# A two-layer decoder trunk on one core: PSUM tiles split by drain time, branch blocks merged in twos, attention one gate sooner, weight units asked for one ahead

## The chip, the core and the metric

The kernel runs on one NeuronCore of a Trainium2 chip. The core has a matrix engine (TensorE, PE in the profile), a vector engine (VectorE, DVE), a scalar engine (ScalarE, ACT), a general engine (GpSimd, POOL), and a queue that starts transfers (SyncE, SP). Each runs its own list of instructions in order and waits on semaphores for the others. Matrix products land in PSUM, which the kernel deals out in tiles of one or two banks; a bank holds 128 x 512 float32 numbers. The metric is the time of one execution on the device, in microseconds (us). It is given as the median of several runs, and beside it stands one profiled execution with its span, the time from its first to its last instruction.

## The reference

Each of two layers is a half-weighted feed-forward block, a mixing block with two branches, and a second feed-forward block. The sequence has 256 positions and the model 1024 features; everything is float32. The chunked selection of key blocks in the full text reduces, at 256 positions and one key block of 256, to causal attention over that block.

```python
def hybrid_layer(x, ...):
    x = x + 0.5 * swiglu(rms_norm(x, ffn1_norm), ffn1_w_gate_up, ffn1_w_down)   # 1024 -> 2 x 2816 -> 1024
    h = rms_norm(x, mix_norm)
    z = h @ w_in                                                                # u, q, k, v: 512 each; gates: 2048
    u, q, k, v, gl = z[..., :o1], z[..., o1:o2], z[..., o2:o3], z[..., o3:o4], z[..., o4:]
    y_pool = multiscale_pool(u, pool_w, pool_scale)      # trailing means over 2, 4, 8, 16 minus u, mapped per group
    q = rope(rms_norm(q.reshape(B, S, N_HEADS, HEAD_DIM), q_norm))              # 8 heads of 64
    k = rope(rms_norm(k.reshape(B, S, N_HEADS, HEAD_DIM), k_norm))
    y_attn = moba_attention(q, k, v)
    gates = jax.nn.sigmoid(gl + b_gate).reshape(B, S, N_BRANCH, D)
    merged = gates[:, :, 0] * (y_pool @ w_branch_pool) + gates[:, :, 1] * (y_attn @ w_branch_attn)
    x = x + merged @ w_out
    return x + 0.5 * swiglu(rms_norm(x, ffn2_norm), ffn2_w_gate_up, ffn2_w_down)
```

## The kernel before

**Numbers.** Every float32 operand of the large products is split into a high part that TensorE's float32r format holds and the rest as a low part. A product is then three: high by high, high by low, low by high. `chain` (L108) makes one 128-block of such a product with two matmuls: the weight's high part against both parts of the activation (N = 512, the two results side by side in one bank), and the weight's low part against the high part (N = 256, added to the first half). A bank thus ends as two halves of 256 columns, and whoever drains it adds them. `drain` (L129) does so: ScalarE copies the second half, and VectorE adds the first.

**Weights.** They come in units of 1 MB (`unit`, L67): SyncE starts a load into one of four `raw` buffers, ScalarE writes the high parts (L91) and VectorE the low parts (L92), in two halves of 128 x 1024, each into one of six `hl` tiles. A call of `unit` brings a unit and returns its halves; for three units before the program's start, loading is written out (L542 to L569), and the calls take these from the list `ahead`.

**PSUM.** The pool `pmm` has two tiles of two banks, `pat` has four of one bank. Waits go by tile: who writes any part of a tile waits for all who had to read an earlier content of any of its parts, and two halves of a tile that are drained at different times hold each other up.

**A layer.** `ffn` (L244): 22 pairs of blocks (`pair`: 32 matmuls into a `pmm` tile, then `drain` into a tile `ab`), each followed by the product with the norm r (L265), the SiLU and a split; then eight output blocks of 22 chains each, added to x by `add_x` (L282). The norm r itself is computed in the middle of the second pair (`norm_all`), or, in the program's first ffn, at the end of three pairs that run together (`pairs`). Then `mix` (L424): q, k, v (`tokens`, `normed`) and the pooling input u; eight gate pairs (`gate`), between which the small work is set; two times four branch blocks, each of 12 matmuls from the pooling branch (`pk`) and 12 from the attention branch (`yk`), merged with the sigmoids of the gates by `merge` (L496) into `mk`; and eight output blocks (w_out). Then the second ffn. The small work among the gates is pooling (`pool`, VectorE and a little GpSimd), the transposes of q and k (`to_features`), the scores and the softmax of four pairs of heads (`scores`), the transposes of the softmax's result (`by_key`, tile pT), and its products with v (`heads_end`). `pl`, `pr`, `pT`, `sq`, `sw`, `ab` and `mg` share one tag of five buffers.

**Order.** TensorE's order is that of the program text (`manual_schedule` for PE). For ScalarE and VectorE a scheduler sets the order when the kernel is built, from the program's order and its own estimates.

The lines that bear on what follows: the two-bank tiles for w_out's first four blocks are

```python
pss = [t[c] for t in big() for c in range(2)]     # 524: outputs 0, 1 in one tile, 2, 3 in the other
```

and in the branch the first four blocks use the same form (L508), the next four a one-bank tile each (L510).

Of the kernel before, what the change touches and what calls it, by code (L numbers as in the profile page):

```python
# [39 lines left out]
def trunk_kernel(ctx: ExitStack, tc: tile.TileContext, x_in, w_in, pw_in, qkn_in, rope_in, mask_in, band_in, out):  # L40
# [178 lines left out]
    def norm_tok():  # L219

        st = pat.tile([P, 2], F32, name="st", tag="at")
        for t in range(2):
            mm(st[:, t:t + 1], lhsT=acc[:, t * P:(t + 1) * P], rhs=ones[:, :1], start=True, stop=True)
        rt = small.tile([P, 2], F32, name="rt", tag="rt", bufs=2)
        rsqrt(rt, st, 1.0 / D)
        return rt

    def spread(rt):
# [3 lines left out]
        halves(dr, dg.rearrange("p a b -> p (a b)"))  # L232
        st = pat.tile([P, S], F32, name="st", tag="at")
        for j in range(2):
# [8 lines left out]

    def ffn(after, first=False):  # L244
        gs = []
# [5 lines left out]
        for i in range(NF):  # L251
# [4 lines left out]
            if first and i == 2:  # L256
                r.append(pairs([unit() for _ in abs_], [t for _, t in abs_], norm_all))
            elif not first and i == 1:
                pair(unit(), ab, NK // 2, lambda: r.append(norm_all()))
            else:  # L260
                pair(unit(), ab)
# [27 lines left out]
    def tokens(pss, mid=None):  # L289

        for kh in range(2):
            hl = unit(tok=True)
            for t in range(2):
                ts = slice(t * P, (t + 1) * P)
                for kk in range(4):
                    k = kh * 4 + kk
                    for c in range(2):
                        z = chunks(hl[kk // 2])[:, kk % 2 * 2 + c]
                        ps = pss[t][c]
                        prod(ps, hx[:, k, 0, ts], z, k == 0, False)  # L300
# [3 lines left out]

    def normed(pss, rt, name):
        z = acts.tile([P, 2, GW], F32, name=name, tag="tok", bufs=3)
        for t in range(2):
            rc = rt[:, t:t + 1]
            for c, ps in enumerate(pss[t]):
                zc = z[:, t, c * S:(c + 1) * S]  # L310
                act(zc, ps[:, 1, :], AF.Copy, scale=rc)
                stt(zc, ps[:, 0, :], rc, zc, op0=OP.mult, op1=OP.add)
        return z
# [110 lines left out]
    def mix(l, after):  # L424
# [21 lines left out]

        ps = big()
        tokens(ps, lambda: box.update(rt=norm_tok()))
        rt = box["rt"]
        q = normed(ps, rt, "q")  # L450
        ps = little()
        tokens(ps)
        k = normed(ps, rt, "k")
        norm_rope(q, qkn[:, l, 0])
        ps = big()
        tokens(ps, lambda: box.update(r=spread(rt)))
        v = normed(ps, rt, "v")
        norm_rope(k, qkn[:, l, 1])
        ps = [pat.tile([P, 2, S], F32, name="pu", tag="at") for _ in range(4)]
        for kh in range(2):  # L460
            hl = unit()
            for kk in range(4):
                i = kh * 4 + kk
                for g in range(4):
                    chain(ps[g], hl, kk * 4 + g, hk[i], i == 0, i == NK - 1)
# [20 lines left out]
        pw = pool_weights(l)  # L486
        gate(5)
        pool_map(pw, d, pk, l)
        gate(6)
        pTs[2] = [by_key(pr) for pr, _ in prs[2]]  # L490
        prs[3] = scores(qT, kT, 3)
        gate(7)
        heads_end(2)
        ei = prs[NP - 1][1][1]

        def merge(f, ps):  # L496
            mg = tmp.tile([P, 2, S], F32, name="mg", tag="t512", bufs=5)
            with tc.issue_after(ei.ins):
                for j in range(2):
                    c = C_BG + j * NK + f  # L500
                    act(gates[:, f, j, :], gates[:, f, j, :], AF.Sigmoid, bias=gain[:, l, c:c + 1])
            tt(mg, ps, gates[:, f], op=OP.mult)  # L502
            tt(mg[:, 0, :], mg[:, 0, :], mg[:, 1, :], op=OP.add)
            halves(mk[f], mg[:, 0, :])

        for f0 in (0, 4):
            if f0 == 0:
                pss = [t[c] for t in big() for c in range(2)]  # L508
            else:
                pss = [pat.tile([P, 2, S], F32, name="ps", tag="at") for _ in range(4)]  # L510
            us = []
            for e in range(4):
                if e % 2 == 0:
                    us.append(unit())
                if f0 == 0 and e == 3:
                    heads_end(3)
                chain3(pss[e][:, 0], us[-1], e % 2 * 8, pk)
                if f0 == 0 and e == 0:
                    pTs[3] = [by_key(pr) for pr, _ in prs[3]]
# [4 lines left out]
        pss = [t[c] for t in big() for c in range(2)]  # L524
        for ks in (range(6), range(6, NK)):
# [44 lines left out]
    for l in range(L):  # L570
        ffn(lambda f: prep(f, l, C_GM), l == 0)
        if l == 0:
# [3 lines left out]
        if l + 1 < L:  # L576
            ffn(lambda f: prep(f, l + 1, C_G1))
        else:
            ffn(lambda f: nc.sync.dma_start(out[:, f, :], x[:, f, :]))

# [89 lines left out]
```

## Time and profile before

| | us |
|---|---|
| median of 3 runs | 1034.88 (1033.51 to 1035.94) |
| the profiled execution | 1032.38 |
| its span | 1030.2 |
| ScalarE busy in the span | 638.7 |
| GpSimd busy in the span | 10.1 |
| transfers, mean share of 16 DMA engines busy by queue q1 | 54.0% |

The profile's lines give an engine, the source line, the operation and the tile written, `<-` the tiles read (numbers left out), the shape, and how often. In the timeline the first two columns are the start and the time in which the group ran, both in us, and a bracket at the end gives the engine's idle time before it and what ended that. The windows give busy time (and number of instructions) of each engine in a stretch, then the granted TensorE clock as a share of full speed, the share of transfers and GB/s. The waits give, for "engine line waited for", the total, the number and the longest wait. The stages of layer 0 are: first ffn to about 190 us, q, k, v and u to about 234, gates and attention to 290, branch blocks to 314.55, output blocks to about 331, then the second ffn; layer 1's mix is at about 696 to 837.

### The profile page before, as it was taken

The numbers are of one execution on the slowest core, as the hardware profiler recorded it, in microseconds if no ns is written. First come the engines' busy times: TensorE is split into PE (matmuls) and PEld (weight loads), VectorE is DVE, ScalarE is ACT, GpSimd is POOL, SyncE is SP. The second block draws the span as 40 slices with busy tenths as digits, with TensorE's granted clock in tenths as the row PEclk, the third lists the DMA queues.
The fourth block names the chain that finished last, engine by engine and source line by source line (L and its number), as shares of the span: only waits on it lengthen the run. The fifth ranks groups of instructions, "written<-read, shape, count | busy, mean of one in ns | idle before, by whom it ended". The sixth has DMA issues, their size and how long they took to land.

```text
span 1030.2 us, 15738 instructions
## 1 busy us (share of the span) xinstructions
PE 1005.6 (98%) x6146; PEld 899.3 (87%) x6146; DVE 822.9 (80%) x1316; ACT 638.7 (62%) x1036; POOL 10.1 (1%) x34
## 2 busy tenths in 40 slices
PE   9899999999997999999999999999999979999998
PEld 7788888888887888899988888888988868999887
DVE  6988866799977888886688887668998779888752
ACT  7766655656775776665566666556577657666541
POOL 0000000002000000000000000000000000000000
PEclk9999999999999999999999999999999999999999
DMA  8765565544634565555555555555464355565540
GB/s 300 256 212 195 200 205 203 170 159 138 235 132 161 194 210 189 190 200 204 205 186 191 196 204 203 197 184 194 137 203 161 123 185 183 205 204 200 201 152 21
DMA packets 30170, 192.88 MB, mean 187 GB/s; under 512 B 3344, under 2 KB 5136, under 8 KB 7568
## 3 DMA queue, kind: packets, MB, share of 16 engines
q1 hardware_dynamic: 30096, 191.88, 54.0%
q8 instruction: 48, 0.79, 0.3%
q14 instruction: 26, 0.21, 0.1%
HBM read 190.82 MB, written 1.05 MB: 186 GB/s over the span
## 4 chain that ended last, share of the span: by engine, by line
PE 95%; DVE 2%; ACT 1%; DMA 1%; issue 0%; SPq 0%; DVEq 0%
PE ps L106 80%; PE pt L106 10%; PE pu L106 2%; DMA raw<-w 1%; PE sc L351 1%; PE pt L375 0%; PE y L385 0%; PE tp L342 0%; ACT hl L91 0%; DVE hl L92 0%; DVE mg L502 0%; ACT t L284 0%; PE yp L106 0%; PE pe L106 0%; DVE gx L286 0%
## 5 line engine op out<-in xcount | busy, mean ns | idle before, releaser
L106 PE MATMUL ps<-hx,hl 128*128 128x512 f32 x3296 | 559.8, 329 | 4.9 <-DVE hl L92 3.9
L106 PEld LDWEIGHTS ps<-hx,hl 128*128 128x128 f32 x3296 | 495.7, 188 | 64.5 <-DVE hl L92 5.8
L92 DVE TENSOR_TENSOR hl<-raw,hl 128x1024 fp32r<-128x1024 f32 (+2 forms) x369 | 441.4, 1199 | 106.7 <-ACT hl L91 106.4
L91 ACT ACTIVATE hl<-raw 128x1024 fp32r<-128x1024 f32 (+2 forms) x369 | 383.1, 1040 | 136.3 <-PE ps L106 88.4
L106 PE MATMUL ps<-ga,hl 128*128 128x512 f32 (+1 forms) x1024 | 176.7, 328 | 0.0
L106 PEld LDWEIGHTS ps<-ga,hl 128*128 128x128 f32 x1024 | 154.0, 188 | 17.5
L130 ACT ACTIVATE ab<-ps 128x512 f32<-128x512 f32 x87 | 51.9, 597 | 98.9 <-PE ps L106 98.7
L131 DVE TENSOR_TENSOR ab<-ps,ab 128x512 f32<-128x512 f32 x87 | 60.1, 691 | 44.4 <-ACT ab L130 44.3
L106 PE MATMUL ps<-gb,hl 128*128 128x512 f32 (+1 forms) x384 | 69.5, 328 | 0.0
L106 PE MATMUL pt<-hl,hx 128*128 128x512 f32 (+1 forms) x384 | 66.3, 331 | 0.0
L106 PEld LDWEIGHTS pt<-hl,hx 128*128 128x128 f32 x384 | 57.7, 187 | 7.3
L267 ACT ACTIVATE sg<-ab 128x256 f32<-128x256 f32 x88 | 36.3, 417 | 43.9 <-DVE ab L265 43.8
L106 PEld LDWEIGHTS ps<-gb,hl 128*128 128x128 f32 x384 | 57.8, 188 | 6.6
L265 DVE TENSOR_TENSOR ab<-ab,r 128x512 f32<-128x512 f32 x88 | 60.5, 692 | 2.4
L106 PE MATMUL pt<-ax,hl 128*128 128x256 f32 (+1 forms) x320 | 47.8, 302 | 13.5 <-DVE gx L286 10.4
L106 PEld LDWEIGHTS pt<-ax,hl 128*128 128x128 f32 x320 | 42.1, 188 | 18.3 <-ACT sq L189 7.8
L106 PE MATMUL ps<-ax,hl 128*128 128x256 f32 (+1 forms) x320 | 45.6, 303 | 0.0
L106 PEld LDWEIGHTS ps<-ax,hl 128*128 128x128 f32 x320 | 42.7, 193 | 2.5
L285 DVE SCALAR_TENSOR_TENSOR t<-t,gx 128x256 f32<-128x256 f32 x48 | 20.3, 422 | 26.1 <-ACT t L284 25.9
L284 ACT ACTIVATE t<-ps 128x256 f32<-128x256 f32 x40 | 15.2, 381 | 37.5 <-PE ps L106 37.4
L268 DVE TENSOR_TENSOR sg<-sg,ab 128x256 f32<-128x256 f32 x88 | 36.6, 420 | 0.0
L181 ACT ACTIVATE hx<-gx 128x256 fp32r<-128x256 f32 x48 | 23.8, 502 | 8.6 <-DVE gx L286 5.8
(127 smaller groups left out, 567.6 us busy)
## 6 DMA issues: line engine op xcount, KB each, us to landing
raw<-w SPq DMA_DIRECT2D x176, 1024.0 KB, 4.9
raw<-w SPq DMA_DIRECT2D x11, 256.0 KB, 6.5
raw<-w SPq DMA_DIRECT2D x2, 512.0 KB, 6.5
out_dram<-gx SPq DMA_DIRECT2D x8, 128.0 KB, 1.9
gx<-x SPq DMA_DIRECT2D x3, 256.0 KB, 6.1
raw<-pw SPq DMA_DIRECT2D x2, 256.0 KB, 2.6
raw<-w SPq DMA_DIRECT2D x2, 128.0 KB, 2.8
qkn<-qkn SPq DMA_DIRECT2D x1, 256.0 KB, 7.8
```

What stands on the lines that cost most here:

```text
L91: act(hi, w, AF.Copy)
L92: tt(lo, w, hi.bitcast(F32), op=OP.subtract)
L106: return mm(steps(ps), lhsT=w, rhs=steps(xk), start=first, stop=last)
L130: act(t, ps[:, :, 1, :], AF.Copy)
L131: tt(t, ps[:, :, 0, :], t, op=OP.add)
L181: act(hx[:, f, 0, :], x[:, f, :], AF.Copy, scale=g)
L265: tt(ab, ab, bc2(r[0]), op=OP.mult)
L267: act(sg, ab[:, 0, :], AF.Silu)
L268: tt(sg, sg, ab[:, 1, :], op=OP.mult)
L284: act(t, ps[:, 1, :], AF.Copy)
L285: stt(t, t, c, x[:, f, :], op0=OP.mult, op1=OP.add)
L351: mm(sc[:, c], lhsT=qT[hs, p, qs], rhs=kT[hs, p, ks], start=True, stop=True)
```

## The change

Four things are changed.

1. *Units asked for one ahead.* `unit` now first calls `ask(2)`, which brings units until two are in the list, and returns the oldest. So the load and the splits of a unit are written into the program one unit sooner than before. The first ffn calls `ask(2)` once more behind its three joint pairs.
2. *Blocks drained at different times get tiles of their own.* q and v move to four tiles of one bank (`little`, `pl`), and k and u to two tiles of two banks (`big`), with u drained two groups at a time. The first four output blocks of w_out get one bank each. The norm's small tiles `st` in `norm_tok` and `spread` come from `pmm`.
3. *Branch blocks merged by twos.* All eight blocks lie two to a two-bank tile. `merge` works on two blocks at once, in place in `gates`, when both are complete.
4. *Attention begins one gate sooner.* The transposes of q and k come ahead of gate 0, scores 0 and 1 behind it, and pooling behind these; the later small work moves up by one gate, and the last `by_key` stands ahead of the branch blocks rather than behind the first.

The place of the norm in the second pair is counted in chains: the same place as before in the second ffns and one chain later in layer 1's first.

```diff
-    def unit(tok=False):
-        if ahead:
-            return ahead.pop(0)
+    LAYER, TOK = 2 * (NF + NF // 2) + 24, range(NF + NF // 2, NF + NF // 2 + 6)
+    def unit():
+        ask(2)
+        return ahead.pop(0)
+    def ask(n):
+        while len(ahead) < n and n_unit[0] < L * LAYER:
+            ahead.append(bring(n_unit[0]))
+            n_unit[0] += 1
+    def bring(u):
         raw, hl = buffers()
-        u = n_unit[0]
-        n_unit[0] += 1
...
-            if tok:
+            if u % LAYER in TOK:
...
         for k in range(NK):
-            if k == at:
-                do()
             for j in range(2):
+                if 2 * k + j == at:
+                    do()
                 chain(ps[:, j], hl, 2 * k + j, hk[k], k == 0, k == NK - 1)
...
-        st = pat.tile([P, 2], F32, name="st", tag="at")
+        st = pmm.tile([P, 2], F32, name="st", tag="mm")
...
                 r.append(pairs([unit() for _ in abs_], [t for _, t in abs_], norm_all))
+                ask(2)
...
         def big():
-            return [[t[:, c] for c in range(2)]
-                    for t in [pmm.tile([P, 2, 2, S], F32, name="pt", tag="mm") for _ in range(2)]]
+            return [pmm.tile([P, 2, 2, S], F32, name="pt", tag="mm") for _ in range(2)]
         def little():
-            return [[pat.tile([P, 2, S], F32, name="pt", tag="at") for _ in range(2)] for _ in range(2)]
+            return [pat.tile([P, 2, S], F32, name="pl", tag="at") for _ in range(4)]
...
-        ps = [pat.tile([P, 2, S], F32, name="pu", tag="at") for _ in range(4)]
+        ps = big()
...
-        for g in range(4):
-            act(u[:, g], ps[g][:, 1, :], AF.Copy)
-            tt(u[:, g], ps[g][:, 0, :], u[:, g], op=OP.add)
-            tt(u[:, g], u[:, g], box["r"], op=OP.mult)
+        for g in (0, 2):
+            z = u[:, g:g + 2]
+            drain(z, ps[g // 2])
+            tt(z, z, bc2(box["r"]), op=OP.mult)
         prs, pTs = {}, {}
-        gate(0)
-        pool(u, d)
         to_features(q, qT)
         to_features(k, kT)
-        gate(1)
+        gate(0)
         for p in (0, 1):
             prs[p] = scores(qT, kT, p)
+        pool(u, d)
+        gate(1)
         gate(2)
-        gate(3)
         for p in (0, 1):
             pTs[p] = [by_key(pr) for pr, _ in prs[p]]
-        gate(4)
+        gate(3)
...
         def merge(f, ps):
-            mg = tmp.tile([P, 2, S], F32, name="mg", tag="t512", bufs=5)
             with tc.issue_after(ei.ins):
-                for j in range(2):
-                    c = C_BG + j * NK + f
-                    act(gates[:, f, j, :], gates[:, f, j, :], AF.Sigmoid, bias=gain[:, l, c:c + 1])
-            tt(mg, ps, gates[:, f], op=OP.mult)
-            tt(mg[:, 0, :], mg[:, 0, :], mg[:, 1, :], op=OP.add)
-            halves(mk[f], mg[:, 0, :])
+                for e in range(2):
+                    for j in range(2):
+                        c = C_BG + j * NK + f + e
+                        act(gates[:, f + e, j, :], gates[:, f + e, j, :], AF.Sigmoid, bias=gain[:, l, c:c + 1])
+            mg = gates[:, f:f + 2]
+            tt(mg, ps, mg, op=OP.mult)
+            tt(mg[:, :, 0, :], mg[:, :, 0, :], mg[:, :, 1, :], op=OP.add)
+            act(ax[:, f:f + 2, 0, :], mg[:, :, 0, :], AF.Copy)
+            tt(ax[:, f:f + 2, 1, :], mg[:, :, 0, :], ax[:, f:f + 2, 0, :].bitcast(F32), op=OP.subtract)
...
             for e in range(4):
-                chain3(pss[e][:, 1], us[e // 2], e % 2 * 8 + 4, yk)
-                merge(f0 + e, pss[e])
+                chain3(pss[e // 2][:, e % 2, 1], us[e // 2], e % 2 * 8 + 4, yk)
+                if e % 2:
+                    merge(f0 + e - 1, pss[e // 2])
         us = [unit() for _ in range(2)]
-        pss = [t[c] for t in big() for c in range(2)]
+        pss = little()
```

The order in which the engines now find their work differs from before at three places that matter here. (Line numbers shift by 9 to 16.) The first is VectorE at the start, at the end of the first ffn's three joint pairs: `hl<-raw` is a weight split, `ab<-ab,r` the product with the norm. Before:

```order
L131 TENSOR_TENSOR ab<-pe,ab 128x256
L265 TENSOR_TENSOR ab<-ab,r 128x512 x3
L92 TENSOR_TENSOR hl<-raw,hl 128x1024
L268 TENSOR_TENSOR sg<-sg,ab 128x256 x2
L131 TENSOR_TENSOR ab<-ps,ab 128x512
```

and now:

```order
L140 TENSOR_TENSOR ab<-pe,ab 128x256
L101 TENSOR_TENSOR hl<-raw,hl 128x1024 x2
L276 TENSOR_TENSOR ab<-ab,r 128x512 x3
L140 TENSOR_TENSOR ab<-ps,ab 128x512
L101 TENSOR_TENSOR hl<-raw,hl 128x1024
L279 TENSOR_TENSOR sg<-sg,ab 128x256 x2
```

Two splits have moved ahead of the three products with r. The second place is ScalarE in layer 0, from the softmax's last exponentials to the transposed weights pT; `ax<-m` is the high part of a pooling difference. Before, all four `ax<-m` stood ahead of the first exponential. Now:

```order
L100 ACTIVATE hl<-raw 128x512
L161 ACTIVATE ax<-m 128x256
L139 ACTIVATE gates<-ps 128x512
L100 ACTIVATE hl<-raw 128x1024
L161 ACTIVATE ax<-m 128x256
L100 ACTIVATE hl<-raw 128x1024
L391 ACTIVATE pT<-pt 128x384
L161 ACTIVATE ax<-m 128x256
L391 ACTIVATE pT<-pt 128x384 x3
L161 ACTIVATE ax<-m 128x256
```

The pooling differences stand among the copies of pT. The third place is VectorE at the last four branch blocks of layer 0. Before (`mg` is the merge's tile, and `ax<-mg` the low part of a merged block):

```order
L502 TENSOR_TENSOR mg<-ps,gates 128x512
L503 TENSOR_TENSOR mg<-mg 128x256
L92 TENSOR_TENSOR hl<-raw,hl 128x1024
L153 TENSOR_TENSOR ax<-mg,ax 128x256
L502 TENSOR_TENSOR mg<-ps,gates 128x512 x2
L503 TENSOR_TENSOR mg<-mg 128x256 x2
L502 TENSOR_TENSOR mg<-ps,gates 128x512
L153 TENSOR_TENSOR ax<-mg,ax 128x256
L503 TENSOR_TENSOR mg<-mg 128x256
L92 TENSOR_TENSOR hl<-raw,hl 128x1024
```

and now:

```order
L101 TENSOR_TENSOR hl<-raw,hl 128x1024 x2
L518 TENSOR_TENSOR gates<-pt,gates 128x1024
L101 TENSOR_TENSOR hl<-raw,hl 128x1024
L519 TENSOR_TENSOR gates<-gates 128x2x256
L518 TENSOR_TENSOR gates<-pt,gates 128x1024
L521 TENSOR_TENSOR ax<-gates,ax 128x2x256
L519 TENSOR_TENSOR gates<-gates 128x2x256
L101 TENSOR_TENSOR hl<-raw,hl 128x1024
L521 TENSOR_TENSOR ax<-gates,ax 128x2x256
```

A block's merge was four instructions of 256 or 512 columns with one split among them; two blocks now take three of 1024 and 512, and two splits stand ahead of the first merge and one behind it.

More of the change, by code (lines that the diff above doesn't have):

```diff
@@ L232, in spread @@
         halves(dr, dg.rearrange("p a b -> p (a b)"))
-        st = pat.tile([P, S], F32, name="st", tag="at")
+        st = pmm.tile([P, S], F32, name="st", tag="mm")
         for j in range(2):
@@ L241, in bc2, with ffn @@
         return a.unsqueeze(1).to_broadcast([P, 2, a.shape[-1]])
-    def ffn(after, first=False):
+    def ffn(after, at=None):
+        first = at is None
         gs = []
@@ L257, in ffn @@
                 r.append(pairs([unit() for _ in abs_], [t for _, t in abs_], norm_all))
+                ask(2)
             elif not first and i == 1:
-                pair(unit(), ab, NK // 2, lambda: r.append(norm_all()))
+                pair(unit(), ab, at, lambda: r.append(norm_all()))
             else:
@@ L291, in tokens @@
         for kh in range(2):
-            hl = unit(tok=True)
+            hl = unit()
             for t in range(2):
@@ L298, in tokens @@
                         z = chunks(hl[kk // 2])[:, kk % 2 * 2 + c]
-                        ps = pss[t][c]
+                        ps = pss[2 * t + c] if len(pss) == 4 else pss[t][:, c]
                         prod(ps, hx[:, k, 0, ts], z, k == 0, False)
@@ L306, in normed @@
         z = acts.tile([P, 2, GW], F32, name=name, tag="tok", bufs=3)
[L307 to L312, printed above, removed]
+        for i, ps in enumerate(pss):
+            n = GW * 2 // len(pss)
+            t = i * n // GW
+            zc, rc = z.rearrange("p t c -> p (t c)")[:, i * n:(i + 1) * n], rt[:, t:t + 1]
+            if n == GW:
+                zc, ps = zc.rearrange("p (c s) -> p c s", s=S), ps.rearrange("p c j s -> p j c s")
+            act(zc, ps[:, 1], AF.Copy, scale=rc)
+            stt(zc, ps[:, 0], rc, zc, op0=OP.mult, op1=OP.add)
         return z
@@ L445, in heads_end @@
             halves(yk[p], values(pTs.pop(p), v, p))
-        ps = big()
+        ps = little()
         tokens(ps, lambda: box.update(rt=norm_tok()))
@@ L450, in mix @@
         q = normed(ps, rt, "q")
-        ps = little()
+        ps = big()
         tokens(ps)
@@ L454, in mix @@
         norm_rope(q, qkn[:, l, 0])
-        ps = big()
+        ps = little()
         tokens(ps, lambda: box.update(r=spread(rt)))
@@ L486, in mix @@
         pw = pool_weights(l)
+        gate(4)
+        pool_map(pw, d, pk, l)
         gate(5)
-        pool_map(pw, d, pk, l)
-        gate(6)
         pTs[2] = [by_key(pr) for pr, _ in prs[2]]
         prs[3] = scores(qT, kT, 3)
+        gate(6)
         gate(7)
         heads_end(2)
+        pTs[3] = [by_key(pr) for pr, _ in prs[3]]
         ei = prs[NP - 1][1][1]
         def merge(f, ps):
-            mg = tmp.tile([P, 2, S], F32, name="mg", tag="t512", bufs=5)
             with tc.issue_after(ei.ins):
-                for j in range(2):
-                    c = C_BG + j * NK + f
-                    act(gates[:, f, j, :], gates[:, f, j, :], AF.Sigmoid, bias=gain[:, l, c:c + 1])
-            tt(mg, ps, gates[:, f], op=OP.mult)
-            tt(mg[:, 0, :], mg[:, 0, :], mg[:, 1, :], op=OP.add)
-            halves(mk[f], mg[:, 0, :])
+                for e in range(2):
[7 more added lines that the diff above has]
+            tt(ax[:, f:f + 2, 1, :], mg[:, :, 0, :], ax[:, f:f + 2, 0, :].bitcast(F32), op=OP.subtract)
         for f0 in (0, 4):
-            if f0 == 0:
-                pss = [t[c] for t in big() for c in range(2)]
-            else:
-                pss = [pat.tile([P, 2, S], F32, name="ps", tag="at") for _ in range(4)]
+            pss = big()
             us = []
@@ L516, in mix @@
                     heads_end(3)
-                chain3(pss[e][:, 0], us[-1], e % 2 * 8, pk)
-                if f0 == 0 and e == 0:
-                    pTs[3] = [by_key(pr) for pr, _ in prs[3]]
+                chain3(pss[e // 2][:, e % 2, 0], us[-1], e % 2 * 8, pk)
             for e in range(4):
-                chain3(pss[e][:, 1], us[e // 2], e % 2 * 8 + 4, yk)
-                merge(f0 + e, pss[e])
+                chain3(pss[e // 2][:, e % 2, 1], us[e // 2], e % 2 * 8 + 4, yk)
+                if e % 2:
+                    merge(f0 + e - 1, pss[e // 2])
         us = [unit() for _ in range(2)]
-        pss = [t[c] for t in big() for c in range(2)]
+        pss = little()
         for ks in (range(6), range(6, NK)):
@@ L570, in trunk_kernel @@
     for l in range(L):
-        ffn(lambda f: prep(f, l, C_GM), l == 0)
+        ffn(lambda f: prep(f, l, C_GM), NK + 1 if l else None)
         if l == 0:
@@ L576, in trunk_kernel @@
         if l + 1 < L:
-            ffn(lambda f: prep(f, l + 1, C_G1))
+            ffn(lambda f: prep(f, l + 1, C_G1), NK)
         else:
-            ffn(lambda f: nc.sync.dma_start(out[:, f, :], x[:, f, :]))
+            ffn(lambda f: nc.sync.dma_start(out[:, f, :], x[:, f, :]), NK)
 def _feat(a):
```

3 lines of the change are left out of this document (2 added, 1 removed).

## The prediction

> **What bounds the kernel now.** The page first: its span, and the busy time of each engine.
>
> ```profile
> span 1030.2 us, 15738 instructions
> PE 1005.6 (98%) x6146; PEld 899.3 (87%) x6146; DVE 822.9 (80%) x1316; ACT 638.7 (62%) x1036; POOL 10.1 (1%) x34
> ```
>
> TensorE (PE) works 1005.6 of 1030.2 us. The diff leaves the matmuls as they are in number and shape, so it can win only from the 24.6 us in which PE stands, and from matmuls that run slowly. The view of waits says what PE stands for; a table of windows says where.
>
> ```profile
> engine line waited for: us in total, times, longest us
> PE pt L106 <- DVE gx L286: 10.4, 4, 3.6
> PE ps L106 <- DVE hl L92: 3.9, 4, 2.4
> PE pt L106 <- DVE mg L502: 3.1, 4, 0.8
> PE pt L375 <- DVE pr L369: 0.8, 2, 0.4
> ```
> ```profile
> core 0: us, PE busy (x) PEld busy (x) DVE busy (x) ACT busy (x) POOL busy (x), PEclk, DMA share, GB/s
> 0.00:36.44 36.44, 30.44 (x161) 25.12 (x162) 28.16 (x55) 29.92 (x56) 1.23 (x22) 1.00 0.75 274
> 36.44:189.84 153.40, 153.40 (x912) 137.47 (x912) 120.91 (x167) 89.69 (x133) 0.00 (x0) 1.00 0.61 209
> ...
> 233.97:290.00 56.03, 56.02 (x370) 49.07 (x368) 54.84 (x130) 39.24 (x86) 5.46 (x6) 1.00 0.52 182
> 290.00:314.55 24.55, 22.61 (x192) 21.81 (x193) 15.74 (x27) 17.66 (x33) 0.00 (x0) 1.00 0.37 130
> 314.55:341.69 27.14, 21.93 (x131) 19.20 (x129) 23.06 (x42) 16.64 (x32) 0.00 (x0) 1.00 0.49 166
> ...
> 796.00:820.80 24.80, 22.84 (x194) 21.92 (x193) 15.99 (x27) 17.79 (x33) 0.00 (x0) 1.00 0.37 129
> 820.80:850.00 29.20, 24.00 (x132) 20.89 (x131) 23.51 (x42) 17.01 (x34) 0.00 (x0) 0.94 0.49 163
> ...
> 1026.00:1030.20 4.20, 0.00 (x0) 0.00 (x0) 0.85 (x2) 0.37 (x1) 0.00 (x0) 0.77 0.09 31
> ```
>
> Length less PE busy, row by row: 6.0 us idle at the start, none in the first ffn, none where attention is prepared (233.97 to 290), 1.94 in the branch blocks, 5.21 in the output blocks; in layer 1 1.96 and 5.20; 4.20 at the end, which the change does not touch. The 233.97 row matters for another reason: VectorE (DVE) works 54.84 of 56.03 us there. PE has no wait, and DVE has almost no slack.
>
> **The output blocks (w_out): -5.2 us in each layer.** The timeline of layer 0:
>
> ```profile
> 314.55 8.93 PE L106 MATMUL pt<-ax,hl 128*128 128x512 f32 x52
> ...
> 323.51 0.39 ACT L284 ACTIVATE t<-pt 128x256 f32<-128x256 f32 x1 [6.61 <-PE pt L106]
> ...
> 323.93 0.42 DVE L285 SCALAR_TENSOR_TENSOR t<-t,gx 128x256 f32<-128x256 f32 x1 [3.40 <-ACT t L284]
> 324.47 0.42 DVE L286 SCALAR_TENSOR_TENSOR gx<-pt,t 128x256 f32<-128x256 f32 x1
> ...
> 325.04 1.58 PE L106 MATMUL pt<-ax,hl 128*128 128x512 f32 x8 [1.56 <-DVE gx L286]
> ...
> 329.70 0.42 DVE L286 SCALAR_TENSOR_TENSOR gx<-pt,t 128x256 f32<-128x256 f32 x1
> ...
> 330.27 0.92 PE L106 MATMUL pt<-ax,hl 128*128 128x512 f32 x4 [3.65 <-DVE gx L286]
> ...
> 331.02 10.83 PE L106 MATMUL ps<-ax,hl 128*128 128x512 f32 x64
> ```
>
> Two outputs share a tile. The last matmuls of the second output wait until DVE has read the first: PE starts again 0.15 us after L286 ends (324.89, 330.12). With four tiles of one bank each, nothing of that is left: 1.56 + 3.65 = 5.21. What is late next is output 4, which takes the first output's bank. One matmul is 8.93/52 = 0.172 us; the first output ends 12 matmuls before output 4 begins, 2.06 us, and its release takes 324.89 - 323.51 = 1.38 us. A split (1.22) in front would make it 2.6. So 0 to 0.5; the order puts no split between, and I take 0.
>
> **The clock: -1.6 us, in layer 1 alone.** The same 64 matmuls behind the same wait:
>
> ```profile
> 836.44 1.01 PE L106 MATMUL pt<-ax,hl 128*128 128x512 f32 x4 [3.64 <-DVE gx L286]
> ...
> 837.26 12.43 PE L106 MATMUL ps<-ax,hl 128*128 128x512 f32 x64
> ```
>
> 12.43 against 10.83 us in layer 0, with the granted clock at 0.94 in that window and 1.00 in layer 0's. After waits of 1.56 and 0.8 us no row is slow. If the longest wait goes, so do these 1.6 us; were they chance, 0 would be won.
>
> The Trainium skill, "TensorE: Matmul & The Clock Gate", Part 1: The HAM clock gate, states that an idle window of about 3.4 us halves the clock, and that the window runs freely. That agrees with two equal waits of which one lost clock. By that rule a wait under 3.4 us costs no clock, and the term stays -1.6; without it the sum would be 1.6 us higher.
>
> **The branch blocks: -1.57, and +1.6 for a new wait.** Before, a second block's matmuls waited for the merge of the first in the same tile:
>
> ```profile
> 298.24 3.01 PE L106 MATMUL pt<-ax,hl 128*128 128x256 f32 x24 [0.78 <-DVE mg L502]
> ...
> 302.04 1.66 PE L106 MATMUL pt<-ax,hl 128*128 128x256 f32 x12 [0.79 <-DVE mg L502]
> ...
> 311.79 2.92 PE L106 MATMUL ps<-ax,hl 128*128 128x256 f32 x24
> ```
>
> Merging when both are done takes these two out. Moving the last key transposes (L375) behind gate 7 takes out 0.39. But the merges end later. The order on DVE at the last blocks is now: split, merge(4,5), split, add, merge(6,7), subtract(4,5). I need durations:
>
> ```profile
> L92 DVE TENSOR_TENSOR hl<-raw,hl 128x1024 fp32r<-128x1024 f32 x32 | 38.7, 1220 | 3.1 <-ACT hl L91 3.1
> L131 DVE TENSOR_TENSOR gates<-ps,gates 128x512 f32<-128x512 f32 x8 | 5.5, 687 | 0.7 <-ACT gates L130 0.6
> L153 DVE TENSOR_TENSOR ax<-m,ax 128x256 fp32r<-128x256 f32 x4 | 1.7, 414 | 0.0
> L91 ACT ACTIVATE hl<-raw 128x1024 fp32r<-128x1024 f32 x33 | 34.9, 1063 | 9.3 <-PE ps L106 4.4 <-PE pu L106 1.6 <-PE pt L106 1.4
> ```
>
> A merge of two is 1024 wide; no such row exists, and I take the split's 1.22 (two of 512 would be 1.37). Count from T, the end of the last branch matmul; one takes 2.92/24 = 0.122 us. The first split's slot is free 36 matmuls before T, at -4.4; ScalarE's copy ends at -3.3, the split at -2.1, merge(4,5) at -0.9, the second split at +0.3, the add (0.69) at 1.0, merge(6,7), which has to wait for T, at 2.2, the subtract at 2.9. PE asks for mk[4] after eight output matmuls, at 1.4. That is a wait of 1.5, with the semaphore 1.6, in each layer. Bounds: 0, if the first split slips behind the merge (then all ends 1.2 sooner, 0.3 left), and 2.8, if one more split stands in front.
>
> **Attention one gate sooner: +0.9 us in each layer.** u is drained in two pieces of 512 (0.69) rather than four of 256 (0.42): some 0.6 us of DVE work less. Pooling moves behind the scores of heads 0 and 1, so its tiles compete with the softmax's and pT's for the five buffers of one tag, and its last ScalarE copies now stand between the pT copies. The values of heads 0 and 1 wait for these. I followed the new order from the end of gate 0. Ahead of the last pool difference stand on DVE six gate products, four softmaxes, three splits and pooling. Neighbours overlap by some 0.08 us (three products of 0.69 take 1.89 in the row at 29.34 below), so this is 6 x 0.60, about 4 x 1.5, 3 x 1.13 and about 5.1, together 18.1 us. PE has the scores (about 1.6) and three gates of 5.4 there, 17.8, and a short hand-over to ScalarE follows. I take 0.5. Scores of head pair 3 wait for a bank that ScalarE empties a little late: 0.3. Gate 0's tile behind the drains of u: 0.1. Bounds of the three: 0, since PE has no idle time to lose here, and 2.2, which is all of pooling's DVE work less one gate. That work is about 7.6 us (3.6 for six L404 adds, four of 512 and two of 256; 3.4 for eight differences and subtracts of 0.42; 0.6 of small ones), and a gate is 32 matmuls of 0.170, 5.4:
>
> ```profile
> 99.84 8.35 PE L106 MATMUL ps<-hx,hl 128*128 128x256 f32 x49
> ...
> 103.85 0.60 ACT L130 ACTIVATE ab<-ps 128x512 f32<-128x512 f32 x1 [1.33 <-PE ps L106]
> ...
> 104.48 0.69 DVE L131 TENSOR_TENSOR ab<-ps,ab 128x512 f32<-128x512 f32 x1 [0.67 <-ACT ab L130]
> ```
>
> **Units asked one ahead: -2.2 us at the start, else nothing.** In the first ffn, the split of the next unit's first half stood on DVE behind three products with r:
>
> ```profile
> 29.34 1.89 DVE L265 TENSOR_TENSOR ab<-ab,r 128x512 f32<-128x512 f32 x3
> ...
> 31.15 1.22 DVE L92 TENSOR_TENSOR hl<-raw,hl 128x1024 fp32r<-128x1024 f32 x1
> ...
> 32.42 2.96 PE L106 MATMUL ps<-hx,hl 128*128 128x256 f32 x16 [2.41 <-DVE hl L92]
> ...
> 36.44 3.74 PE L106 MATMUL ps<-hx,hl 128*128 128x256 f32 x21 [1.05 <-DVE hl L92]
> ```
>
> Now it stands ahead of them: done at 29.4 + 1.2 = 30.6 rather than 32.37. PE is free at 32.42 - 2.41 = 30.0, and its wait falls to about 0.8; two of 0.2 follow, as the displaced products delay the next splits. 3.46 becomes 1.2. Bounds: 0 to 3.46 left. In the ffns' steady part the order on ScalarE and DVE is as it was. A pair's drain ends 105.17 - 103.85 = 1.3 us after the pair, and the tile is wanted a pair later (5.4), so 4.1 us of delay, three splits, would cost nothing there. On SyncE's queue one weight load passes the three small loads of rope, mask and gains, and one passes the pooling weights. The DMA share there is 0.5 to 0.6, no row of PE waits for a load, and I count both at nothing. ffn2's norm a little later or earlier in its pair is covered by the same pair.
>
> **Sum.** Each layer: -5.21 - 1.57 - 0.39 + 1.6 + 0.9 = -4.7. Twice, -9.3; the clock -1.6; the start -2.2: -13.1. The profiled execution took 1032.38 us (span 1030.2), so 1019.3. The runs shown have a median of 1034.88, 2.5 above it; on that base 1021.8, say **1022.0 us**.
>
> **The rivals.** *The new waits are two to three times as long.* For it: DVE at 54.84 of 56.03, where each late step delays all behind it. Against: the chains were followed with measured durations. 2.5 a layer becomes 5: +5, about 1027; chance 0.18, from 1025 to 1031. *They do not come at all*, because the scheduler's order leaves slack that I count as used: -5, and -1 at the start, 1016; chance 0.08. *The change buys nothing*: the output blocks find another wait of about 5 us, such as mk[4] behind two more splits and the sigmoids. 1032 to 1036; against it stands that DVE itself idles 3.40 us in these blocks; chance 0.05. *Slower: pooling gets onto the path.* Place: the values of heads 0 and 1. If the five shared buffers tie the transposed weights to the end of pooling and gates 1 and 2 cover nothing, the wait is 7.6 rather than 0.5 in each layer, +14.2, and at a wait of that length 1.6 more is lost in each layer, as in the 837.26 row: +3.2. 1021.8 + 17.4 = 1039. It decides from a wait of about 7 us on. Against: those gates are 10.9 us of cover, and three of pooling's four results stand ahead of most of the copies. Chance 0.03.
>
> **How the numbers follow.** The forecast (1018.5 to 1025) has 0.66; the rivals 0.18, 0.08, 0.05, 0.03. Less than 0.2%, about 2 us, can't be told from no change here. Faster: 0.66 + 0.18 + 0.08 = 0.92; same 0.05; slower 0.03. The range leaves out the slow third of the first rival and most of the small ones: 1017 to 1029. The bounds of the terms, 0 to 5 us of new waits in each layer and 0 to 3.5 at the start, reach from 1015.6 to 1029.
>
> **What would show it.** Right: no PE wait for gx and none for mg or gates' merges by line in the branch; one of 1 to 2 us for ax (the subtract) early in the output blocks; granted clock 1.00 in layer 1's output blocks; DVE's split at 29.4 and a PE wait under 1 us there. Wrong: a PE wait over 2 us at the values of heads 0 and 1 or at a gate; PE busy over 1006 us; or any PE idle time in the steady ffns.

## The result, and the profile after

The changed kernel takes 1018.89 us in the median (1017.31 to 1019.39, 4 runs), the kernel before 1034.22 beside it; the ratio is 0.9847, with a 95% interval of 0.9829 to 0.9864. That is about 15 us faster, more than the 12.9 forecast and within the range. Six more runs of it, shown below, gave 0.987 (0.9846 to 0.9895). Its profiled execution took 1018.97 us, 13.4 less than that of before.

The page of the changed kernel begins:

```profile
span 1016.9 us, 15687 instructions
PE 1003.9 (99%) x6146; PEld 899.3 (88%) x6146; DVE 815.6 (80%) x1280; ACT 636.0 (63%) x1020; POOL 8.0 (1%) x34
```

PE works 1.7 us less, and stands 13.0 us instead of 24.6. What it waits for, by the view of waits (engine, line, waited for; total us, number, longest):

```profile
PE ps L115 <- DVE hx L191: 3.5, 4, 1.3
PE pl L115 <- DVE ax L521: 3.1, 2, 1.5
PE ps L115 <- DVE hl L101: 1.2, 3, 0.7
```

The rows for gx (10.4), for the branch merges (3.1) and for the key transposes (0.8) are gone. The row for ax is the wait that the prediction worked out, 1.54 us in each layer. The first row was not foreseen. Layer by layer, with windows (length, busy time of PE, PEld, DVE, ACT, POOL, then granted clock, share of transfers, GB/s):

```profile
228.00:284.00 56.00, 56.00 (x359) 48.87 (x359) 53.38 (x123) 41.51 (x89) 3.59 (x6) 1.00 0.51 174
284.00:308.03 24.03, 24.03 (x212) 23.42 (x209) 15.56 (x19) 16.43 (x28) 0.00 (x0) 1.00 0.48 170
308.03:331.21 23.18, 21.64 (x131) 19.21 (x129) 18.41 (x33) 14.46 (x27) 0.00 (x0) 1.00 0.40 137
331.21:345.00 13.79, 12.06 (x62) 10.11 (x61) 12.10 (x20) 8.21 (x14) 0.00 (x0) 0.88 0.73 238
810.76:833.94 23.18, 21.64 (x130) 19.21 (x129) 18.41 (x33) 14.46 (x27) 0.00 (x0) 1.00 0.40 139
833.94:847.73 13.79, 12.05 (x71) 10.33 (x70) 13.08 (x21) 9.74 (x16) 0.00 (x0) 1.00 0.76 250
```

Attention (first row) and the branch blocks (second) run without any idle time of PE. The output blocks (308.03 to 331.21) lose 1.54 us, the start of the second ffn (from 331.21) 1.73; layer 1 does the same. In each layer PE thus stands 3.27 us in place of 7.15. PE's own timeline there, in layer 0 and, behind the dots, in layer 1:

```profile
311.08 9.63 PE L115 MATMUL pl<-ax,hl 128*128 128x512 f32 x56 [1.54 <-DVE ax L521]
...
335.84 0.94 PE L115 MATMUL ps<-hx,hl 128*128 128x512 f32 x4 [0.47 <-DVE hx L191]
338.04 5.27 PE L115 MATMUL ps<-hx,hl 128*128 128x512 f32 x20 [1.26 <-DVE hx L191]
...
838.58 0.94 PE L115 MATMUL ps<-hx,hl 128*128 128x512 f32 x4 [0.48 <-DVE hx L191]
840.78 3.64 PE L115 MATMUL ps<-hx,hl 128*128 128x512 f32 x20 [1.26 <-DVE hx L191]
```

`hx` of features 6 and 7 is the second ffn's input. It is made from w_out's last two outputs, on ScalarE and VectorE, and PE now arrives before it. The two layers differ in one thing: the same 20 matmuls take 5.27 us in layer 0 and 3.64 in layer 1. In layer 0 the clock was halved, for 3.41 us:

```profile
334.86:338.27 3.41, 1.68 (x9) 1.04 (x8) 3.41 (x8) 1.68 (x3) 0.00 (x0) 1.00 0.65 216
338.27:341.68 3.41, 3.41 (x12) 2.82 (x12) 3.03 (x5) 1.96 (x3) 0.00 (x0) 0.50 0.63 207
```

The start of the program, where two splits now stand ahead of the products with r:

```profile
28.97 2.35 DVE L101 TENSOR_TENSOR hl<-raw,hl 128x1024 fp32r<-128x1024 f32 x2
...
30.24 2.97 PE L115 MATMUL ps<-hx,hl 128*128 128x256 f32 x16 [0.69 <-DVE hl L101]
...
31.24 1.89 DVE L276 TENSOR_TENSOR ab<-ab,r 128x512 f32<-128x512 f32 x3
```

One wait of 0.69 is left of 2.41 and 1.05.

### The profile page after: what moved, and what is told of

It reads as the page before. It is cut to its first block, busy times and chain, and to the rows that moved or that the text cites. A ratio compares the mean times of both kernels' runs of the same rounds, so it can differ in the third digit from the quotient of the medians.

```text
span 1016.9 us, 15687 instructions
## 1 busy us (share of the span) xinstructions
PE 1003.9 (99%) x6146; PEld 899.3 (88%) x6146; DVE 815.6 (80%) x1280; ACT 636.0 (63%) x1020; POOL 8.0 (1%) x34
## 3 DMA queue, kind: packets, MB, share of 16 engines
HBM read 190.82 MB, written 1.05 MB: 189 GB/s over the span
## 4 chain that ended last, share of the span: by engine, by line
PE 92%; DVE 5%; issue 1%; ACT 1%; DMA 1%; SPq 0%; DVEq 0%
PE ps L115 76%; PE pt L115 8%; PE pl L115 6%; DVE hl L101 2%; PE sc L365 1%; PE y L399 1%; DMA raw<-w 1%; PE pt L389 1%; DVE hx L191 1%; ACT hl L100 0%; DVE gx L297 0%; DVE gates L518 0%; DVE acc L199 0%; DVE t L296 0%; PE tp L356 0%
## 5 line engine op out<-in xcount | busy, mean ns | idle before, releaser
L115 PE MATMUL pt<-ax,hl 128*128 128x256 f32 x384 | 45.0, 277 | 0.0
L115 PE MATMUL pl<-hl,hx 128*128 128x512 f32 (+1 forms) x256 | 44.9, 331 | 0.0
L115 PEld LDWEIGHTS pt<-ax,hl 128*128 128x128 f32 x384 | 44.3, 188 | 0.3 <-issue 0.3
L115 PEld LDWEIGHTS pl<-hl,hx 128*128 128x128 f32 x256 | 38.5, 188 | 4.8
L161 ACT ACTIVATE ga<-sg 128x256 fp32r<-128x256 f32 x64 | 25.5, 406 | 5.5 <-DVE sg L279 5.4
L162 DVE TENSOR_TENSOR ga<-sg,ga 128x256 fp32r<-128x256 f32 x64 | 26.3, 418 | 0.0
```

The lines of the kernel that those rows point to most:

```text
L115: return mm(steps(ps), lhsT=w, rhs=steps(xk), start=first, stop=last)
L161: act(d[:, 0, :], v, AF.Copy)
L162: tt(d[:, 1, :], v, d[:, 0, :].bitcast(F32), op=OP.subtract)
```

## The experiments

Two theories stood against each other. By the first, the gain is a sum of waits, each stage for itself, and own tiles for w_out carry most of it. By the second, the parts need each other: the order, the splits ahead and the merges by twos make the room without which own tiles would only meet another wait. Times are medians in us. The kernel before ran beside each group of kernels (1034.83, 1033.9 and 1034.94), and ratios are to it.

**Own tiles undone.** Changed kernel, with

```diff
-        pss = little()
+        pss = [t[:, c] for t in big() for c in range(2)]
```

> The changed kernel with one thing undone: the first four output blocks share two-bank tiles again. Theory (the gain is a sum of stages): the waits for gx come back, 1.56 and 3.65 us in each layer, and the wait for hx at the start of the second ffn (1.73 in each layer now) goes, because VectorE gets the time back; net 2 x (5.2 - 1.7) = +7 us, about 1026 against 1018.9. Rival (the later merges and the new order had already removed most of that wait, and own tiles are worth little): the gx waits come to under 2 us in each layer and the time stays within 3 us of 1018.9.

Measured: 1032.87, ratio 0.9986 (0.9964 to 1.0009). Its waits:

```profile
PE pt L115 <- DVE gx L297: 10.4, 4, 3.6
PE pt L115 <- DVE ax L521: 3.1, 2, 1.5
```

The waits came back to the digit, and the hx waits went: +6.9 by waits (13.5 against 6.6), as expected. But the time rose by 14, twice that, which neither theory nor rival had. The mean granted clock of its ten runs was 0.9947; that of the changed kernel's first four was 0.999, a difference of 4.4 us over the span. Its profile shows low clock at the longest gx wait (3.6) in each layer, 0.83 and 0.77 in these two windows:

```profile
330.00:340.00 10.00, 9.40 (x47) 8.36 (x48) 8.84 (x18) 6.57 (x13) 0.00 (x0) 0.83 0.58 205
...
830.00:840.00 10.00, 4.94 (x19) 4.11 (x20) 8.97 (x17) 7.74 (x15) 0.00 (x0) 0.77 0.31 107
```

So the other parts together, without own tiles, show no gain that can be measured. Of the 14 us, 2.7 are left beside waits and clock. What makes them is not shown; in this kernel's profile the first ffn ran at the slowest of the paces that the last section tells of.

**Own tiles alone.** Kernel before, with

```diff
-        pss = [t[c] for t in big() for c in range(2)]
+        pss = [pat.tile([P, 2, S], F32, name="ps", tag="at") for _ in range(4)]
```

(at w_out only)

> The kernel before with one thing done: the first four output blocks of w_out get one-bank tiles of their own. Theory: the gx waits (5.2 in each layer) go, and a wait for hx of about 1.7 takes their place, with units asked for when needed as before; some wait for the last merges is possible because the one-bank tiles are the branch's too. Net -2 x 3.5 = -7 us, about 1027 against 1034.2. Rival (hx waits only because of the splits ahead): no hx wait, -10 us or more, 1024 or less. Rival (own tiles only move the wait to the bank that the merges still hold): 2 us or less are won.

Measured: 1023.73, ratio 0.9895 (0.9876 to 0.9914), -11 us.

```profile
PE pt L106 <- DVE mg L502: 3.1, 4, 0.8
PE ps L106 <- DVE hx L182: 3.0, 3, 1.3
```

This one line is worth about seven tenths of the change (11 of 15 us). Waits for hx take the place of part of the gx waits although no unit is asked for ahead, so the rival that blames the splits ahead falls. By waits alone -7.4 was due (10.4 - 3.0), so again some 4 us more were won; the mean clock is 0.9988 against 0.9942 for the runs of before beside it, which is 4.7 us over the span.

**No unit ahead.** Changed kernel, with

```diff
     def unit():
-        ask(2)
+        ask(1)
         return ahead.pop(0)
...
-                ask(2)
```

> The changed kernel with one thing undone: units are asked for when needed, as before. Theory: the start loses its gain, PE waits of 2.4 and 1.05 us for a split come back there (+2.8 us); the wait for hx at the start of the second ffn stays at about 1.7 in each layer, because it comes from output blocks that follow each other without a pause. About 1021.7. Rival for the hx wait (the splits asked for ahead stand in front of add_x on VectorE): it goes to under 0.3 in each layer, so the time is 1018 or less, +2.8 - 3.5.

Measured: 1022.82, ratio 0.9891 (0.9873 to 0.9908), +3.9 against the changed kernel's 1018.89.

```profile
PE ps L115 <- DVE hl L101: 3.6, 2, 2.6
PE pl L115 <- DVE ax L520: 3.2, 2, 1.6
PE ps L115 <- DVE hx L191: 3.1, 4, 1.3
```

The start's waits are back (2.57 and 1.05), and the waits for hx are 3.1 in place of 3.5. Asking ahead is worth the start, 2.4 us by its waits (3.6 against 1.2), and does nothing to hx.

**Merging by ones.** Changed kernel, with merges of one block each on the same two-bank tiles:

```diff
-                if e % 2:
-                    merge(f0 + e - 1, pss[e // 2])
+                merge(f0 + e, pss[e // 2][:, e % 2])
```

(and `merge` as it was before, in place in `gates`)

> The changed kernel with one thing undone: each branch block is merged by itself, still two to a two-bank tile. Theory (merging by twos trades waits for waits): in each of the four tiles of a layer the second block waits 0.8 us for the first one's product, 3.1 in each layer, and the wait for ax (1.54 in each layer) falls to about 0.3; net 2 x 1.9 = +4 us, about 1022.5. Rival (twos bought nothing, the split in front of the merge is what counts): the wait for ax stays at 1.5 or the new ones are hidden; within 1.5 us of 1018.9.

Measured: 1029.47, ratio 0.9949 (0.9931 to 0.9968): +10.6, where +4 was expected.

```profile
PE pt L115 <- DVE gates L517: 10.2, 8, 1.8
PE ps L115 <- DVE hx L191: 3.8, 5, 1.3
```

The wait for ax is gone, as expected, but of the four merge waits in a layer two are 0.78 and two are 1.75 to 1.82, since a split now stands on VectorE ahead of the merge that PE waits for. Waits account for 7.1 to 7.4 of the 10.6. In the two profiles PE's busy time differs by another 2.6 (1006.5 against 1003.9): the first ffn ran at the slowest pace here too. Once all blocks lie in two-bank tiles, merging by twos is needed; against the layout of before, with four blocks in tiles of their own, it only trades 1.57 for 1.54.

**The old order of attention.** Changed kernel, with the sequence from `gate(0)` to `heads_end(2)` as in the kernel before, and the last `by_key` behind the first branch block:

```diff
-        to_features(q, qT)
-        to_features(k, kT)
         gate(0)
-        for p in (0, 1):
-            prs[p] = scores(qT, kT, p)
         pool(u, d)
+        to_features(q, qT)
+        to_features(k, kT)
         gate(1)
+        for p in (0, 1):
+            prs[p] = scores(qT, kT, p)
...
```

> The changed kernel with one thing undone: the order of gates, attention and pooling of before, with the last key transposes behind the first branch block. Theory (that order cost one wait of 0.39 in each layer, and moving it is worth only that): +0.8 us, 1019 to 1020.5; no wait of PE over 1 us between the gates. Rival (attention one gate sooner carries the gain in that stage, and with the new tiles the old order waits): +3 us or more, with PE waits among gates 0 to 4.

Measured: 1025.54, ratio 0.9888 (0.9851 to 0.9925), with runs from 1019.9 to 1027.6.

```profile
PE ps L115 <- DVE qk L140: 2.9, 2, 1.5
PE pt L389 <- DVE pr L383: 0.8, 2, 0.4
```

The rival is the nearer one: it had the new tiles as the cause, though not which. Gate 0 comes straight behind u, and u now lies in the two tiles that gate 0 needs; it waits 1.45 to 1.49 until VectorE has drained u. With the transposes of q and k between them, nothing waits. So the new order saves 3.7 us of waits in both layers together, most of which u's new tiles would otherwise cost. The medians are 6.7 apart, but the runs overlap those of the changed kernel, which reach 1023.57 in a later group, so the time alone shows no more than the waits do.

Both theories are thus right in part. Own tiles for w_out need none of the other parts: alone they win 11.1. The others without them win 2.0, which lies within the noise, and the two together are 13.1 of the 15.3. But some of the other parts need each other: without merging by twos, two-bank tiles for all branch blocks lose 10.6, and with the old order u's new tiles cost 2.9 at gate 0.

**Cutting w_out at four and four.** In the changed kernel's timeline VectorE idles in the output blocks, just ahead of the first chain to hx:

```profile
319.16 0.43 DVE L296 SCALAR_TENSOR_TENSOR t<-t,gx 128x256 f32<-128x256 f32 x1 [4.66 <-ACT t L295]
```

With the wait for ax this suggested one more line:

```diff
-        for ks in (range(6), range(6, NK)):
+        for ks in (range(4), range(4, NK)):
```

> The changed kernel with the first four output blocks cut at four and four chains rather than six and two. Theory: merged block 4 is asked for after 32 output matmuls (5.5 us) rather than 8, so the wait for ax (1.54 in each layer) goes to 0; the first outputs end 2 us sooner and 1.4 us apart, VectorE's idle stretch of 4.7 us there is used, and the wait for hx falls from 1.73 to 0.5 or less. Net -2 x (1.5 + 1.2) = -5.5 us, and no slow clock: about 1013 to 1014. Rival (VectorE sets the end of the output blocks): what is saved at ax comes back at hx, which grows to 3 us in each layer, and the time stays within 1 us of 1018.9.

Measured: 1014.71, ratio 0.9809 (0.9788 to 0.983); the mean clock of its four runs is 1.000.

```profile
PE ps L115 <- DVE hx L191: 2.3, 2, 1.1
```

That is 4.2 less than the changed kernel, where 5.5 was expected. The wait for ax is gone, and hx falls to 1.15 in each layer, less far than expected. VectorE takes 2.5 us for each output there, as two neighbouring rows of its timeline show, so that an earlier start reaches the last output only in part:

```profile
330.92 0.47 DVE L191 SCALAR_TENSOR_TENSOR hx<-gx,hx 128x256 fp32r<-128x256 f32 x1
...
333.45 0.47 DVE L191 SCALAR_TENSOR_TENSOR hx<-gx,hx 128x256 fp32r<-128x256 f32 x1
```

**Two pairs together.** On top of that, the first two pairs of the second ffn:

```diff
+        for ks in (range(6), range(6, NK)):
+            for n, (hl, ps) in enumerate(zip(ws, pss)):
+                if ks[0] and n:
+                    do()
+                for k in ks:
+                    for j in range(2):
+                        chain(ps[:, j], hl, 2 * k + j, hk[k], k == 0, k == NK - 1)
```

> The four-four kernel with one thing more: the first two pairs of the second ffn run together, features 0 to 5 of both before 6 and 7 of either. Theory (the wait for hx there is for the last two outputs of w_out, which VectorE finishes late): the first use of features 6 and 7 moves from 4.1 to 8.2 us after the last output block, and the wait of 1.15 in each layer goes to 0; about 1012.5 against 1014.7. Rival (VectorE is behind by more than that, or the norm becomes late): a wait of the same length stands at the norm or at the second pair, and the time stays within 1 us of 1014.7.

Measured: 1013.48, ratio 0.9798 (0.9772 to 0.9823). No wait for hx and none for the norm is left, in either layer; PE stands only at the start and the end. That is 2.3 us less waiting. The median is 1.2 us lower, and 2.4 lower in the later group, below; the four-four kernel ran in neither of these groups, and the intervals of the ratios overlap, so the gain is shown by the waits and not by the time.

**Filling the waits of before.** To see what idle time does to the clock, matmuls whose results nobody reads were set ahead of the chains that wait in before's output blocks:

```diff
+                if ks[0] and e % 2:
+                    busy = pat.tile([P, P], F32, name="busy", tag="at")
+                    for _ in range(3 if e == 1 else 7):
+                        mm(busy, lhsT=ones, rhs=ones, start=True, stop=True)
```

> The kernel before, with matmuls whose result nobody reads filling its waits in the output blocks: three of 0.48 us in the wait of 1.56 and seven in the wait of 3.65, so that PE works there without being held up longer. Theory (idle PE is what slows the clock, and the runs of before lose more to it, mean granted clock 0.994 over 13 runs, than its profiled execution did, 0.997): the mean granted clock rises to about 0.998, the waits of the other matmuls stay as long, and the time falls by 1.5 to 4 us, to 1031 to 1033.3 against 1034.8. Rival (the slow clock has nothing to do with these waits): clock and time as before, within 1 us.

Measured: 1033.78, ratio 0.9999 (0.9982 to 1.0016), mean clock 0.9973 over ten runs. One matmul took 0.22 us, not 0.48, so 0.90 and 2.07 us of waiting remained; and a split had moved ahead on VectorE, so that hx waited 0.8 in each layer. The clock rose from 0.9946 of before beside it, and the time did not fall; with the new wait for hx of 1.6 in all, this kernel decides nothing. The next one has 7 and 16 of these matmuls:

> The kernel before with longer filling of its waits in the output blocks: 7 and 16 matmuls of 0.22 us (the shorter filling showed 0.22 for one, and left waits of 0.9 and 2.07; it also put one weight split ahead on VectorE, which cost a wait for hx of 0.8 in each layer). Theory (idle PE slows the clock): the mean granted clock of the runs rises from 0.9944 (27 runs) to 0.998 or more, and the time falls by that, 3.6 us and more, less the 1.6 for hx: about 1032.4 against 1034.4. Rival (the clock falls for another reason): the clock stays at 0.994 to 0.995 and the time is 1034 or more.

Measured: 1031.80 (12 runs), ratio 0.9973 (0.996 to 0.9985), mean clock 0.9983 against 0.9939 for the 17 runs of before beside it.

```profile
PE pt L106 <- DVE mg L502: 3.1, 4, 0.8
PE ps L106 <- DVE hl L92: 2.9, 3, 2.4
PE pt L106 <- DVE gx L286: 2.1, 2, 1.1
```

The wait for hx that the shorter filling had caused is not there. The output blocks became longer, since one more split now stands on VectorE in the chain that ends the wait. From their first matmul to output 4 they take 17.50 and 17.45 us, where before took 16.47 (314.55 to 331.02) and 16.58:

```profile
313.75 8.97 PE L106 MATMUL pt<-ax,hl 128*128 128x512 f32 x52
...
331.25 10.87 PE L106 MATMUL ps<-ax,hl 128*128 128x512 f32 x64
...
821.06 8.92 PE L106 MATMUL pt<-ax,hl 128*128 128x512 f32 x52
...
838.51 10.88 PE L106 MATMUL ps<-ax,hl 128*128 128x512 f32 x64
```

In before's profile the clock was halved behind the longest of these waits in layer 1; here it is 1.00 at both places. (In this profile it is low once, 0.83 from 30 to 40 us, behind the start's wait of 2.4; the second wait for a split there, 1.05 before, is not met in it.) So nothing useful was added or made shorter there, 1.9 us were lost, and the kernel still became about 3 us faster. Idle PE slows the clock, and the slow clock has a price beside the wait.

**The changed kernel and the two-pairs kernel again**, for the spread:

> The changed kernel once more, for its clock and its pace over more executions. Theory (the profiled execution of before stood for too little slow clock): mean granted clock 0.998 to 0.9995 against 0.994 of the runs of before beside it, so about 4.5 us of the gain are clock and the rest waits; ratio 0.983 to 0.987. Theory of the pace (a stretch of matmuls without a pause runs at one of three paces, drawn anew at a pause, so that the same kernel differs between executions): of its four feed-forward stages at least one shows 5.55 or 5.63 us for 32 matmuls, where the first profile of this kernel had 5.50 in all. Rival (the pace belongs to the kernel): 5.50 in all four again.

Measured: 1020.69 (6 runs from 1018.48 to 1023.57), ratio 0.987 (0.9846 to 0.9895), mean clock 0.9993. The clock came as expected. All four ffn stages of the profile ran at 5.50 again, so the pace part was not met here, although two runs with a clock of 1.000 lie 4 us apart (1018.48 and 1022.72).

> The kernel with four-four output blocks and two joint pairs once more. Theory (its profile ran the first feed-forward block at 5.63 us for 32 matmuls and the second at 5.55, by chance): this profile has other paces, and the median of more runs lies 1 to 2.5 us below that of the four-four kernel (1014.7); mean clock 0.999 or more. Rival (pace belongs to the kernel): 5.63 and 5.55 again in the same stages, and a time of 1013.5 as before.

Measured: 1012.35, ratio 0.9784 (0.9763 to 0.9806). The two profiles of this kernel differ in the first layer's second ffn. Here is first that of the earlier run, at its output blocks (start, us, PE, matmuls):

```profile
451.74 5.55 PE L115 MATMUL ps<-ga,hl 128*128 128x512 f32 x32
457.13 2.18 PE L115 MATMUL ps<-gb,hl 128*128 128x512 f32 x12
```

and the same place in the later run:

```profile
450.72 5.50 PE L115 MATMUL ps<-ga,hl 128*128 128x512 f32 x32
456.06 2.16 PE L115 MATMUL ps<-gb,hl 128*128 128x512 f32 x12
```

The first ffn ran at 5.63 in both. So the pace of a stage can differ between executions of one kernel; that it is drawn anew each time is not shown.

## Why the prediction was right, and where it was not

*Output blocks, -5.2 in each layer:* right. The gx rows are gone, and return exactly when the tiles are shared again. The step "what is late next" was wrong: it looked at output 4's bank alone, and had no term for the second ffn's first pair. Late next was hx of the last two outputs, 1.73 us in each layer. PE came 5 us earlier, and VectorE's chain behind the last outputs did not.

*Branch blocks, -1.57 + 1.6:* right in both terms; the ax wait measured 1.54.

*Attention, +0.9 in each layer:* wrong. No wait stands there. The count of VectorE's work, 18.1 against 17.8 us, took all of it as in the way; the profile has 53.38 busy of 56.00, which is 2.6 us of slack where 1.2 had been. And the 0.1 for gate 0 does not show that this place costs 1.47 with the old order.

*Start, -2.2:* the mechanism right, the size small: 3.46 fell to 0.69, -2.8. The first split began at 28.97, not 29.4, and the two later waits of 0.2 did not come.

*Clock, -1.6 in layer 1 alone:* the term that was mis-sized. The profiled executions show one halved stretch each, layer 1 before and layer 0 after, so between them nothing was won. But over 44 runs of before the mean granted clock is 0.9942 (0.991 to 0.997; the profiled one had 0.997), and over ten of the changed kernel 0.9992. That difference times the span is 5 us, an upper estimate, since the clock also falls in the last 4 us, where no matmul runs (0.77 in before's last window). The filled kernel puts some 3 us on it by time, and some 5 with the 1.9 us by which its output blocks became longer. In the sum this is the step from the profiled execution to the runs: it added 2.5 to both kernels. The runs of before do lie that much above its profile; the changed kernel's first four do not (1018.89 against 1018.97), and the later six lie 1.7 above it.

Together, in the profiled executions: 2 x 3.9 less waiting in the layers and 3.7 at the start make 11.5. Of the start's 3.7, 2.8 are the splits. The other 0.9 are waits for the first weights, in the first 8 us, which the first profile of the changed kernel does not have. Its second profile has 1.3 of them, so they are not the change's. PE's busy time fell by 1.7, of which the clock is nothing. The first ffn of both layers ran at a slower pace before than after (last section); counted from the traces, that is 2.7 us of PE's time, and 1.0 was lost elsewhere. That the forecast of -13.1 met -13.4 there was in part luck, since errors cancelled: attention was 1.8 too dear, 3.5 for hx were forgotten, 1.6 for the clock were not won there, and loads and pace were not foreseen. Against the runs the clock was counted too low.

The Trainium skill's page "TensorE: Matmul & The Clock Gate", Part 1: The HAM clock gate, gave the forecast "a wait under 3.4 us costs no clock". Here the measurement decides otherwise: two waits, of 0.47 and 1.26 us, within one stretch of 3.41 us in which PE worked 1.68, were followed by 3.41 us at half the clock. The length 3.41 agrees with the window that the page states. In layer 1 the same waits cost nothing, which fits its statement that the windows run freely.

None of the rivals came. "They do not come at all" was right for attention alone.

## What to carry to other kernels

When a wait on the busiest engine goes, follow every chain that starts in the freed stage to its next reader, not only the buffer in question: here it was the next block's input that became late. A tile that is drained in two pieces at different times, while someone writes the second, is the first thing to look for; one line was some seven tenths of this change. And time a change by several runs: the profiled execution of before had less of the slow clock than most of its runs.

## What the runs showed of the hardware

*The clock falls on less idle time than the forecast had.* Mean granted clocks by PE's longest wait behind the program's start: 0.9942 with 3.65 us (before, 44 runs), 0.9947 with 3.65 (own tiles undone, 10), 0.9973 with the waits filled to 2.08 (10), 0.9983 with them filled to 1.06 (12), 0.9992 with 1.54 (the changed kernel, 10), 1.000 with 1.15 (four and four, 4). The halved stretch behind the two waits for hx is no single case: the profile without a unit ahead has one of 3.41 us at 342.86, that of the old attention at 845.28. How little work is too little is not settled. In before's profile two stretches of 3.41 us, from 325.12 and from 328.53, hold 1.50 and 1.67 us of PE work around the longest wait in layer 0, and the clock stays at 1.00 behind both.

*At a granted clock of 1.00 TensorE runs at more than one pace.* 32 matmuls of the ffn's output blocks took 5.50, 5.55 or 5.63 us, and each of the ffn stages holds one of these from its first output to its last: eight groups, one value, in every stage of every profile. In 13 profiles with four stages each, 36 stages are at 5.50, 12 at 5.55 and 4, all of them the program's first ffn, at 5.63. Before had 5.55 in the first ffn of both layers and 5.50 in the second; these rows are the first and the second ffn of layer 0.

```profile
130.59 5.55 PE L106 MATMUL ps<-ga,hl 128*128 128x512 f32 x32
...
459.29 5.50 PE L106 MATMUL ps<-ga,hl 128*128 128x512 f32 x32
```

5.55 against 5.50 is 0.9%, by estimate 1.6 us in a stage of 176; so much more PE works in before's first ffn of layer 1 than in the changed kernel's. 5.63 is 2.4%; where it stands and the clock is 1.00, PE works 2.6 to 3.2 us more up to the end of the first ffn (three profiles against the changed kernel's). This is of the size of the spread between runs of one kernel at a clock of 1.000, and may be it. What sets the pace stays open.
